# Differential attention: the low part of q in a doubled 128-row layout for the second pass of the score product

## The chip, the cores and the metric

The kernel runs on one core of a Trainium2 chip. The metric is the device time of one execution in microseconds (us); lower is better. Five engines work side by side and meet only through semaphores: TensorE (PE, with its weight loads listed as PEld), VectorE (DVE), ScalarE (ACT), GpSimd (POOL) and SyncE (SP, which issues most DMAs).

## What is computed

The reference is a four-layer trunk over 512 latent and 256 context tokens of width 1024. Layers 0 and 3 mix tokens with a short gated convolution, layer 1 with windowed attention, layer 2 with differential attention; each is followed by a gated convolutional feed-forward. Only layer 2's attention is touched here. It has 8 heads, each with two queries and two keys (index c) of 64 channels and one value of 128:

```python
s = jnp.einsum("bqhcd,bkhcd->bhcqk", q_j, keys, preferred_element_type=F32) * scale
p = jax.nn.softmax(s, axis=-1)
a = (p[:, :, 0] - lam * p[:, :, 1]).astype(vals.dtype)
o = jnp.einsum("bhqk,bkhe->bqhe", a, vals)
return rmsnorm(o, sub_g) * (1.0 - lam_init)
```

The 512 latent queries read 768 keys (512 latent, 256 context).

## The kernel before

All products run in the matmul type fp32r. To keep float32 accuracy each operand is split into a high part (the value cast to fp32r) and a low part (the value less the high part), and a product is the sum of high by high, high by low and low by high, three matmuls into one PSUM tile (`mm3`, lines 160 to 162). Where the contraction has only 64 channels, as in the scores, two of the three are put into one matmul of 128 rows.

That is what `diff_attn` does. `kT` holds, for each head and each c, a 128-row block with the 768 keys along the free axis: rows 0 to 63 carry one part of the key and rows 64 to 127 the other (high then low for c = 0, low then high for c = 1). `qprep(hd, tt)` makes the matching stationary operands for one head and one block of 128 queries. ACT copies the two high parts, each twice (`qst`, line 949), POOL forms the two low parts (line 950), PE transposes three 128x128 blocks into the PSUM tile `pqt` (line 953), and ACT copies them to `qT` (line 955): block 0 is the high part of query 0 doubled, block 1 that of query 1 doubled, block 2 the two low parts stacked, each in the 64 rows where the key's high part lies.

`scores(v)` (v is a head and a half of the queries, 16 in all, two query blocks each) then makes four score tiles `psS` [128 queries, 768 keys], 64 in the whole layer. A tile takes four matmuls: 512 keys by the 128-row high operand (line 979), the same keys by the 64-row low operand (line 980), and both again for the last 256 keys. Behind a tile come the row maximum on DVE (line 982), the exponential with its row sum on ACT (line 984), and after both c of a query block the scaling and the sum of the two on POOL (lines 993 and 994, the second listed under helper line 156). The PSUM pool has two buffers for `psS` and four of one bank for everything else.

`values(v)` transposes the combined probabilities on PE (line 1008), splits them on ACT and DVE (lines 1013 and 1014) and multiplies them with the values (`pO`, lines 160 to 162). `finish` normalizes a head (`oss` line 1041, `ops` line 176) and `out_proj` adds its output product (`pd`, lines 160 to 162 and 430). `timeline` weaves these generators; the order in which each engine then runs its instructions is fixed at build time by the scheduler of the language. PE, DVE, ACT and POOL take their instructions in that order.

`setup` makes two identity matrices, `ident` in float32 and `identr`, a cast of it to fp32r (lines 203 to 206).

Of the kernel before, what the change touches and what calls it, by code (L numbers as in the profile page):

```python
# [9 lines left out]
F32 = mybir.dt.float32  # L10
F32R = mybir.dt.float32r
AF = mybir.ActivationFunctionType
ALU = mybir.AluOpType
# [32 lines left out]
class Trunk:  # L46
# [1 line left out]
        self.tc, self.nc, self.A, self.out, self.stop = tc, tc.nc, A, out, stop  # L48
        self.xside = "left"

    # ---------------------------------------------------------------- weights
    def plan_weights(self):
        A = self.A
        w = []
# [55 lines left out]
        return hi, lo  # L110

    def prefetch(self, n):
        """Splits the next n weights, one a step, and lifts the limit."""
        for _ in range(n):
            if len(self.wready) < self.wpos + 5:
                self._split(True)
            self.wlimit = max(self.wlimit, len(self.wready))
            yield
# [10 lines left out]
        self.wready[i] = None  # L129
        return r  # L130

    # ---------------------------------------------------------------- helpers
    def ps(self, name):
        return self.pp.tile([P, 1024], F32, name=name, tag="ps", bufs=2)

# [40 lines left out]
            self.nc.tensor.matmul(ps[:, t * P:(t + 1) * P], r[:, t:t + 1].to_broadcast([P, P]), self.ident,  # L176
                                  start=True, stop=True)

    # ---------------------------------------------------------------- setup
    def setup(self, es):  # L180
        tc, nc, A = self.tc, self.nc, self.A
        self.cp = cp = es.enter_context(tc.tile_pool(name="const", bufs=1))
        self.pp = es.enter_context(tc.tile_pool(name="psum", bufs=1, space=PSUM))
        self.WR, self.WS = 3, 5
        self.wpool = es.enter_context(tc.tile_pool(name="w", bufs=1))

        pk = cp.tile([P, self.A["pack"].shape[1]], F32, name="pack")
        nc.sync.dma_start(pk, self.A["pack"])
        pos = 0

        def take(*dims):
            nonlocal pos
            n = math.prod(dims)
            v = pk[:, pos:pos + n]
            pos += n
            if len(dims) == 2:
                return v.rearrange("p (a b) -> p a b", b=dims[1])
            return v

        craw = take(KC, 2)  # L200
        self.cpair = cp.tile([P, KC, 2], F32, name="csilu")
        nc.scalar.activation(self.cpair, craw, AF.Silu)
        self.ident = cp.tile([P, P], F32, name="ident")
        make_identity(nc, self.ident)
        self.identr = cp.tile([P, P], F32R, name="identr")
        nc.vector.tensor_copy(self.identr, self.ident)
        self.ones = cp.tile([P, P], F32, name="ones")
        nc.gpsimd.memset(self.ones, 1.0)
        self.mhalf = cp.tile([P, 8], F32, name="mhalf")
        nc.gpsimd.memset(self.mhalf, -0.5)  # L210

        self.ada_b = [take(6, KC) for _ in range(DEPTH)]
        self.g1 = [take(KC) for _ in range(DEPTH)]
        self.g2 = [take(KC) for _ in range(DEPTH)]
        self.fcw = [take(NF, 3) for _ in range(DEPTH)]
        self.fcb = [take(NF) for _ in range(DEPTH)]
        self.scw = {l: take(KC, 3) for l in (0, 3)}
        self.sink = take(16)
        self.subln = take(1)
        self.mods = {}  # L220
        for l in range(DEPTH):
            for s in ((0, 1) if l < 3 else (0,)):
                self.mods[l, s] = cp.tile([P, 6, KC], F32, name=f"mod{l}_{s}")
        hL = [cp.tile([P, SEQ], F32, name=f"hL{k}") for k in range(KC)]
        self.hC2 = [cp.tile([P, 2, CTX], F32, name=f"hC{k}") for k in range(KC // 2)]
        hC = [self.hC2[k // 2][:, k % 2, :] for k in range(KC)]
        self.h = {0: hL, 1: hC}
# [4 lines left out]
        for k in range(KC):  # L232
            self.tc.keep_in_program_order(self.nc.sync.dma_start(self.h[0][k], self.A["x"][k]))

    # ---------------------------------------------------------------- ada
    def ada_vecs(self, l, m):
        return (0, 1) if l < 2 or (l == 2 and m < 2) else (0,)

    def ada_first(self):
        """Shift and scale of the first norms: a chunk of channels at a time, straight on the tensor engine."""  # L240
        nc = self.nc
        for j in range(KC):
            if j in EARLY:
# [62 lines left out]
            if next(self.ada, "end") == "end":  # L306
                break

    # ---------------------------------------------------------------- norm
    def norm_steps(self, l, s, second, first):  # L310
        """RMS norm and modulation of one stream: a step for the square of each chunk, then the rest.
        The first norms scale the chunks by the statistics before the modulation is there."""
        nc = self.nc
        sid, T, off = s
        xp = self.xp
# [67 lines left out]
            if k % 2 or first:  # L383
                yield

    # ---------------------------------------------------------------- pair structure
    def project(self, src, xn, parts, name, acc=None, split=False):
        """Projects some parts of the streams; acc is what an earlier call for other parts returned."""
        if acc is None:
            if split:  # L390
                out = {sid: self.pb(name) for sid, _, _ in parts}
            else:
                ps = self.ps(name)
                out = {0: ps[:, :SEQ], 1: ps[:, SEQ:TOK], "all": ps}
            acc = self.get_w(src), out
        (wh, wl), out = acc
        for s in parts:
            sid, T, off = s
            o = out[sid][:, off:off + T]
            for k in range(KC):  # L400
                xh, xl = xn[s][k]
                w = slice(k * P, (k + 1) * P)
                self.mm3(o, wh[:, w], wl[:, w], xh, xl, k == 0, k == KC - 1)
        return acc

    def phase_start(self, srcs, xn, regions):
        """The first projections of a phase leave the last part of the streams to the end."""
        n = PRM["nb"] if len(regions) == 2 else PRM["nl"]
        self.pre = [self.project(src, xn, parts_of(regions)[:-1], f"pre{i}", split=i >= 2) for i, src in enumerate(srcs[:n])]

# [20 lines left out]
                    yield  # L431

    def begin(self, s, first=False):
        """The norm of stream s for the phase that follows, if it takes part there."""
        if self.next is None or s not in parts_of(self.next[1]):
            return iter(())
        if self.xn_next is None:
# [3 lines left out]
        return self.norm_steps(self.next[0], s, self.next[2], first)  # L441

    def boundary(self, seq, gate, before=()):
        """The last down products, stream by stream, woven with the norms of the next phase."""
        prev = list(before)
        for s, units, ws, last in seq:
            nrm = self.begin(s) if last else iter(())
# [12 lines left out]
                pass  # L460

    def timeline(self, tasks, rate):
        """Interleaves generators: each task (begin, end, steps, generator) takes its steps evenly over its slots,
        and the filler takes rate steps a slot."""
        live = []
        tasks = sorted(tasks, key=lambda t: t[0])
        at, due, end = 0, 0.0, max(t[1] for t in tasks)
# [61 lines left out]

    @staticmethod  # L530
    def pair_order(n):
        """Units go up and down in groups, each going down while the next goes up; the last four go down together."""
        order = []
        for g in range(0, n - 2, GRP):
            order += [("up", c) for c in range(g, g + GRP)]
# [69 lines left out]
        gate = {sid: self.mods[l, sid][:, 2, :] for sid, _, _ in streams}  # L605
        self.pairs(KC, up, A[f"l{l}_sc_out"], gate, streams, ticks)

    # ---------------------------------------------------------------- attention pieces
    def rope_table(self, l, which, yt):
        """Gain, and cosine and sine with the gain in them, of one of q and k."""  # L610
        nc, A = self.nc, self.A
        g = yt.tile([P, 2, HD], F32, name=f"gain{l}{which}")
        nc.sync.dma_start(g, A[f"l{l}_gain"][:, "qk".index(which)])
# [58 lines left out]
                mm(o, xh, wl[:, w], start=False, stop=k == KC - 1)  # L672
            post(tt, o)

    # ---------------------------------------------------------------- layer 1 mixer
    def window_gqa(self, xn):
        nc, A = self.nc, self.A
        yc = self.tc.tile_pool(name="y1", bufs=1, side=self.yside)
# [203 lines left out]
        self.boundary([(H1, final[H1], ws[1], True)], gate, [nrm, nrm0])  # L882
        mc.__exit__(None, None, None)

    # ---------------------------------------------------------------- layer 2 mixer
    def diff_attn(self, xn):
        nc, A = self.nc, self.A
        yc = self.tc.tile_pool(name="y2", bufs=1, side=self.yside)
# [54 lines left out]
            yield  # L943

        def qprep(hd, tt):
            st = xb.tile([P, 3, 2, HD], F32R, name="qst", tag="qst", bufs=2)
            qc = (hd % 4) * P
            q3 = qraw[hd // 4, tt][:, qc:qc + P].rearrange("p (c d) -> p c d", c=2)
            self.cpy("st", st[:, 0:2], q3[:, :, None, :].to_broadcast([P, 2, 2, HD]))
            self.tt("stl", st[:, 2], q3, st[:, 0:2, 0, :].bitcast(F32), ALU.subtract)  # L950
            pt = self.pb("pqt")
            for c in range(3):
                self.tr(pt[:, c * P:(c + 1) * P], st[:, c].rearrange("p a d -> p (a d)"))
            qT = xb.tile([P, 3, P], F32R, name="qT", tag="qT", bufs=2)
            self.cpy("qT2", qT, pt[:, :384].rearrange("p (c t) -> p c t", c=3))
            return qT

        def scores(v):
# [9 lines left out]
            for n in range(2):  # L968
# [4 lines left out]
                pts = []  # L973
                for c in range(2):
                    s = self.ps("psS")
                    hs = slice(c * HD, c * HD + HD)
                    for a, b in ((0, 512), (512, 768)):
                        kt = kT[hd // 4][:, 2 * (hd % 4) + c, a:b]
                        nc.tensor.matmul(s[:, a:b], qT[:, c, :], kt, start=True, stop=False)  # L979
                        nc.tensor.matmul(s[:, a:b], qT[hs, 2, :], kt[hs], start=False, stop=True)  # L980
                    nm = self.small(1, "nm")
                    nc.vector.tensor_reduce(nm, s[:, :TOK], axis=AX.X, op=ALU.max, negate=True)
                    p = xb.tile([P, TOK], F32, name="pP", tag="P", bufs=6)
# [119 lines left out]
        self.boundary([(s, *self.last, True) for s in (H0, H1)], gate)  # L1103
        mc.__exit__(None, None, None)

    # ---------------------------------------------------------------- whole
    def run(self):
        tc, nc = self.tc, self.nc
        es = ExitStack()
# [183 lines left out]
```

## Time and profile before

| | |
|---|---|
| Time, median of 3 runs | 3337.18 us (3334.94 to 3341.43) |
| Span of the profiled execution, first to last instruction | 3339.3 us |
| Time of the profiled execution itself | not listed apart from its span |
| Mean granted TensorE clock | 0.972 of full |
| Score, softmax and value stage of layer 2 | about 2135 to 2365 us of the span |

A profile row of a timeline gives the start, the busy time, the engine, the line of the kernel, the operation, the tiles (out<-in), the shape and how many instructions are merged. Busy times of PE overlap, because a matmul is counted until its result is written; the distance from one start to the next is what a matmul costs the queue. In brackets stands the idle time of the engine before the row and what ended it; "issue" means that nothing seen in the profile did.

### The profile page before, as it was taken

How to read it: one execution, taken by the hardware profiler on the slowest of the kernel's cores; microseconds unless marked ns; L12 is line 12 of the kernel's file. 1: busy time of each engine (PE TensorE's matmuls, PEld its weight loads, DVE VectorE, ACT ScalarE, POOL GpSimd, SP SyncE). 2: the span in 40 equal slices, each digit the busy share in tenths (PEclk: the TensorE clock that was granted, in tenths of full speed). 3: DMA queues.
4: the chain of work that ended last, by engine and by line, in shares of the span. 5: the costliest groups of instructions: out<-in, count | busy, mean ns of one | idle time of the engine just before them, and what ended most of it. 6: DMA issues, size and time to landing. Idle time of an engine off the chain costs nothing.

```text
span 3339.3 us, 53917 instructions
## 1 busy us (share of the span) xinstructions
PE 3272.2 (98%) x22364; PEld 2979.7 (89%) x22364; DVE 2207.4 (66%) x3278; ACT 1127.0 (34%) x1888; POOL 686.3 (21%) x578
## 2 busy tenths in 40 slices
PE   8999999999998999999999999999999999999999
PEld 7999999989986778999999987677899999999999
DVE  5775887786565676676666576366687765565555
ACT  4113322222333565422222243356432323242222
POOL 2132223211132333111000134255211110010000
PEclk9999999999996899899999999899999999999999
DMA  6431443442110000333333112401265532222322
GB/s 226 139 108 52 152 132 110 134 132 77 52 65 19 14 21 6 102 108 113 110 127 112 60 54 79 142 29 54 68 202 161 179 112 89 95 89 84 101 89 76
DMA packets 105237, 323.29 MB, mean 97 GB/s; under 512 B 12576, under 2 KB 27552, under 8 KB 104992
## 3 DMA queue, kind: packets, MB, share of 16 engines
q1 hardware_dynamic: 100512, 313.26, 29.0%
q0 software_dynamic: 4480, 6.58, 0.9%
q8 instruction: 176, 2.88, 0.3%
q14 instruction: 69, 0.57, 0.1%
HBM read 311.26 MB, written 8.53 MB: 96 GB/s over the span
## 4 chain that ended last, share of the span: by engine, by line
PE 93%; DVE 4%; ACT 1%; DMA 1%; issue 1%; POOL 0%; SPq 0%; ACTq 0%; DVEq 0%; POOLq 0%
PE pd L160 8%; PE pd L161 8%; PE pd L162 8%; PE pa L161 6%; PE pa L160 6%; PE pa L162 6%; PE pg L160 6%; PE pg L162 6%; PE pg L161 6%; PE pj L670 3%; PE pj L671 3%; PE pj L672 3%; PE psS L980 2%; PE pO L826 2%; PE pPT L816 1%; PE psS L979 1%
## 5 line engine op out<-in xcount | busy, mean ns | idle before, releaser
L108 ACT CAST wh<-wr 128x1024 fp32r<-128x1024 f32 x380 | 392.2, 1049 | 1282.1 <-issue 524.9
L109 DVE TENSOR_TENSOR wl<-wr,wh 128x1024 fp32r<-128x1024 f32 x380 | 497.9, 1323 | 233.0 <-ACT wh L108 231.6
L160 PE MATMUL pd<-mh,wh 128*128 128x256 f32 (+1 forms) x1712 | 568.6, 333 | 9.9 <-DVE hC L430 9.2
L161 PE MATMUL pd<-ml,wh 128*128 128x256 f32 (+1 forms) x1712 | 564.1, 330 | 0.3 <-DVE ml L1057 0.3
L162 PE MATMUL pd<-mh,wl 128*128 128x256 f32 (+1 forms) x1712 | 563.7, 329 | 0.0
L430 DVE SCALAR_TENSOR_TENSOR hL<-pd,mod,hL 128x512 f32<-128x512 f32 (+1 forms) x512 | 335.6, 660 | 249.7 <-PE pd L162 248.2
L160 PE MATMUL pg<-xh,wh 128*128 128x256 f32 x1648 | 465.5, 282 | 1.5 <-ACT gp L575 1.5
L162 PE MATMUL pg<-xh,wl 128*128 128x256 f32 x1648 | 465.3, 282 | 0.0
L162 PE MATMUL pa<-xh,wl 128*128 128x256 f32 x1648 | 465.3, 282 | 0.0
L160 PE MATMUL pa<-xh,wh 128*128 128x256 f32 x1648 | 465.3, 282 | 0.0
L161 PE MATMUL pa<-xl,wh 128*128 128x256 f32 x1648 | 465.3, 282 | 0.0
L161 PE MATMUL pg<-xl,wh 128*128 128x256 f32 x1648 | 465.2, 282 | 0.0
L291 POOL PARTITION_ALL_REDUCE acc<-acc x34 | 222.9, 6587 | 1130.8 <-DVE acc L289 1130.8
L160 PEld LDWEIGHTS pd<-mh,wh 128*128 128x128 f32 x1712 | 325.8, 190 | 39.0 <-DVE hC L430 9.6
L162 PEld LDWEIGHTS pd<-mh,wl 128*128 128x128 f32 x1712 | 326.4, 191 | 30.8
L161 PEld LDWEIGHTS pd<-ml,wh 128*128 128x128 f32 x1712 | 326.4, 191 | 25.6 <-DVE ml L1057 0.5
L289 DVE SCALAR_TENSOR_TENSOR acc<-adaw,csilu,acc 128x1024 f32<-128x1024 f32 x238 | 297.8, 1279 | 47.5 <-DMA adaw<-l_ada_w 44.5
L160 PEld LDWEIGHTS pg<-xh,wh 128*128 128x128 f32 x1648 | 314.1, 191 | 5.5 <-ACT gp L575 1.7
L161 PEld LDWEIGHTS pg<-xl,wh 128*128 128x128 f32 x1648 | 314.0, 191 | 4.3
L162 PEld LDWEIGHTS pg<-xh,wl 128*128 128x128 f32 x1648 | 314.2, 191 | 2.1
L160 PEld LDWEIGHTS pa<-xh,wh 128*128 128x128 f32 x1648 | 314.6, 191 | 0.1
L161 PEld LDWEIGHTS pa<-xl,wh 128*128 128x128 f32 x1648 | 314.6, 191 | 0.1
(234 smaller groups left out, 6311.9 us busy)
## 6 DMA issues: line engine op xcount, KB each, us to landing
adaw<-l_ada_w SPq DMA_DIRECT2D x176, 512.0 KB, 3.7
wr<-l_ffn_up SPq DMA_DIRECT2D x176, 512.0 KB, 3.6
wr<-l_ffn_down SPq DMA_DIRECT2D x88, 512.0 KB, 3.6
wr<-l_sc_in SPq DMA_DIRECT2D x48, 512.0 KB, 3.6
wr<-l_da_qkv SPq DMA_DIRECT2D x24, 512.0 KB, 3.9
adaf<-l_ada_first SPq DMA_DIRECT2D x16, 512.0 KB, 5.7
wr<-l_sc_out SPq DMA_DIRECT2D x16, 512.0 KB, 3.6
wr<-l_wa_qkv SPq DMA_DIRECT2D x12, 512.0 KB, 3.8
```

The costliest lines, as they stand in the source:

```text
L108: keep(self.nc.scalar.copy(hi, raw))
L109: keep(self.nc.vector.tensor_tensor(lo, raw, hi.bitcast(F32), ALU.subtract))
L160: mm(ps, wh, xh, start=first, stop=False)
L161: mm(ps, wh, xl, start=False, stop=False)
L162: mm(ps, wl, xh, start=False, stop=last)
L289: keep(nc.vector.scalar_tensor_tensor(acc[v], raw, c, acc[v], ALU.mult, ALU.add))
L291: nc.gpsimd.partition_all_reduce(acc[v], acc[v], P, bass.bass_isa.ReduceOp.add)
L430: nc.vector.scalar_tensor_tensor(hk, ps, gate[sid][:, oc:oc + 1], hk, ALU.mult, ALU.add)
L670: mm(o, xh, wh[:, w], start=k == 0, stop=False)
L671: mm(o, xl, wh[:, w], start=False, stop=False)
L672: mm(o, xh, wl[:, w], start=False, stop=k == KC - 1)
L826: nc.tensor.matmul(po, vw, t, start=n == 1 and i == 0, stop=n == len(keys) and i == 1)
```

## The change

`qprep` makes the low parts in the same doubled form as the high parts: POOL writes 128x256 elements in place of 128x128, PE transposes four blocks in place of three, and ACT copies 512 columns in place of 384. Blocks 2 and 3 of `qT` are now the low part of query 0 and of query 1, each in both halves of the rows. `scores` uses them over all 128 rows of `kT`, so that the product of the low parts is added to the score too. Apart from that `setup` no longer keeps a float32 identity: it builds one in a scratch tile, casts it to `identr`, and reads `identr` as float32 where `ident` was read. Each of the two `qst` buffers and each of the two `qT` buffers grows by 512 bytes a partition; the dropped identity frees 512. The diff also removes comments and docstrings, left out here.

```diff
@@ setup
-        self.ident = cp.tile([P, P], F32, name="ident")
-        make_identity(nc, self.ident)
+        eye = self.ntmp("eye")[:, :P]
+        make_identity(nc, eye)
         self.identr = cp.tile([P, P], F32R, name="identr")
-        nc.vector.tensor_copy(self.identr, self.ident)
+        nc.vector.tensor_copy(self.identr, eye)
+        self.ident = self.identr.bitcast(F32)
@@ qprep
-            st = xb.tile([P, 3, 2, HD], F32R, name="qst", tag="qst", bufs=2)
+            st = xb.tile([P, 4, 2, HD], F32R, name="qst", tag="qst", bufs=2)
...
-            self.cpy("st", st[:, 0:2], q3[:, :, None, :].to_broadcast([P, 2, 2, HD]))
-            self.tt("stl", st[:, 2], q3, st[:, 0:2, 0, :].bitcast(F32), ALU.subtract)
+            q4 = q3[:, :, None, :].to_broadcast([P, 2, 2, HD])
+            self.cpy("st", st[:, 0:2], q4)
+            self.tt("stl", st[:, 2:4], q4, st[:, 0:2].bitcast(F32), ALU.subtract)
             pt = self.pb("pqt")
-            for c in range(3):
+            for c in range(4):
                 self.tr(pt[:, c * P:(c + 1) * P], st[:, c].rearrange("p a d -> p (a d)"))
-            qT = xb.tile([P, 3, P], F32R, name="qT", tag="qT", bufs=2)
-            self.cpy("qT2", qT, pt[:, :384].rearrange("p (c t) -> p c t", c=3))
+            qT = xb.tile([P, 4, P], F32R, name="qT", tag="qT", bufs=2)
+            self.cpy("qT2", qT, pt.rearrange("p (c t) -> p c t", c=4))
@@ scores
-                    hs = slice(c * HD, c * HD + HD)
                     for a, b in ((0, 512), (512, 768)):
                         kt = kT[hd // 4][:, 2 * (hd % 4) + c, a:b]
                         nc.tensor.matmul(s[:, a:b], qT[:, c, :], kt, start=True, stop=False)
-                        nc.tensor.matmul(s[:, a:b], qT[hs, 2, :], kt[hs], start=False, stop=True)
+                        nc.tensor.matmul(s[:, a:b], qT[:, 2 + c, :], kt, start=False, stop=True)
```

## Rows read from the trace of the kernel before

**Rows 1.** The page's busy shares: us, share of the span, instructions.

```profile
PE 3272.2 (98%) x22364; PEld 2979.7 (89%) x22364; DVE 2207.4 (66%) x3278; ACT 1127.0 (34%) x1888; POOL 686.3 (21%) x578
```

**Rows 2.** Windows of layer 2's attention: length, busy by engine, granted clock, DMA share, GB/s.

```profile
2135.00:2160.00 25.00, 20.20 (x46) 10.26 (x46) 9.83 (x16) 10.65 (x24) 11.11 (x15) 0.55 0.50 159
2160.00:2200.00 40.00, 39.37 (x159) 27.71 (x159) 19.13 (x36) 22.33 (x49) 20.71 (x21) 0.73 0.08 20
2200.00:2350.00 150.00, 148.43 (x782) 108.10 (x783) 100.98 (x170) 88.28 (x190) 83.33 (x81) 1.00 0.14 41
```

**Rows 3.** Waits from 2200 to 2350 us: total, times, longest.

```profile
DVE nm L982 <- PE psS L980: 23.6, 33, 2.1
PE oss L1041 <- ACT osq L1037: 1.6, 2, 0.8
```

**Rows 4.** Timeline of PE around one score tile at full clock.

```profile
2200.59 0.48 PE L979 MATMUL psS<-kT,qT 128*128 128x512 f32 x1
2201.01 0.49 PE L980 MATMUL psS<-kT,qT 64*128 64x512 f32 x1
2201.43 0.39 PE L979 MATMUL psS<-kT,qT 128*128 128x256 f32 x1
2201.74 0.38 PE L980 MATMUL psS<-kT,qT 64*128 64x256 f32 x1
2202.05 0.45 PE L165 MATMUL pqt<-identr,qst 128*128 128x128 f32 x3
2202.34 0.35 PE L160 MATMUL pO<-aTh,vhl 128*128 128x256 f32 x1
2202.53 0.28 PE L161 MATMUL pO<-aTl,vhl 128*128 128x256 f32 x1
2202.65 0.28 PE L162 MATMUL pO<-aTh,vl 128*128 128x256 f32 x1
```

**Rows 5.** Timeline of the weight loads (PEld) in the same stretch.

```profile
2201.01 0.18 PEld L980 LDWEIGHTS psS<-kT,qT 64*128 64x128 f32 x1 [0.25 <-issue]
...
2202.53 0.19 PEld L162 LDWEIGHTS pO<-aTh,vl 128*128 128x128 f32 x1
```

**Rows 6.** Timeline of PE: two matmuls of 512 columns with 128 rows.

```profile
2288.31 0.39 PE L160 MATMUL pd<-mh,wh 128*128 128x512 f32 x1
2288.54 0.40 PE L161 MATMUL pd<-ml,wh 128*128 128x512 f32 x1
```

**Rows 7.** Timeline of PE at half clock: two score tiles' first matmuls, two of 128 rows.

```profile
2154.36 0.79 PE L979 MATMUL psS<-kT,qT 128*128 128x512 f32 x1
...
2156.83 0.79 PE L979 MATMUL psS<-kT,qT 128*128 128x512 f32 x1
...
2167.36 0.41 PE L160 MATMUL pO<-aTh,vhl 128*128 128x256 f32 x1
2167.57 0.41 PE L161 MATMUL pO<-aTl,vhl 128*128 128x256 f32 x1
```

**Rows 8.** Groups of ACT from 2200 to 2350 us: busy, mean ns, idle before.

```profile
L1013 ACT CAST aTh<-pPT 128x512 fp32r<-128x512 f32 x33 | 19.3, 588 | 13.4 <-PE pPT L1008 13.1
L151 ACT CAST qT<-pqt 128x384 fp32r<-128x384 f32 x22 | 10.6, 481 | 16.0 <-PE pqt L165 16.0
```

**Rows 9.** Groups of POOL from 2200 to 2350 us.

```profile
L156 POOL TENSOR_TENSOR pP<-pP 128x768 f32<-128x768 f32 x23 | 42.1, 1830 | 1.3
L156 POOL TENSOR_TENSOR qst<-qraw,qst 128x128 fp32r<-128x128 f32 x16 | 7.4, 461 | 20.6 <-ACT qst L151 20.5
```

**Rows 10.** Timelines of ACT and PE: a PSUM buffer's release and its next use.

```profile
2258.23 0.21 ACT L984 ACTIVATION_READ_ACCUMULATOR pP<-psS,nm 128x1 f32 x1
...
2258.49 0.50 PE L979 MATMUL psS<-kT,qT 128*128 128x512 f32 x1
```

**Rows 11.** Windows of layer 1's attention, columns as in rows 2.

```profile
1030.00:1045.00 15.00, 15.00 (x39) 9.41 (x39) 6.12 (x16) 5.13 (x14) 2.71 (x4) 0.50 0.00 0
1165.00:1180.00 15.00, 14.75 (x90) 11.43 (x90) 11.90 (x28) 9.21 (x23) 5.14 (x6) 1.00 0.00 1
```

## The prediction on record

> **What bounds the kernel now.** I read the page's busy shares first: PE is busy 98% of the span and nothing else is near it [rows 1], so whatever shortens PE's queue anywhere should shorten the whole, if the queue doesn't start to wait. Then the windows of the stage that the change touches. From 2200 to 2350 us PE is busy 148.4 of 150 us at full clock, with DVE at 67%, ACT at 59% and POOL at 56%; the 65 us before that run partly at half clock (granted 0.55 and 0.73) [rows 2]. From these shares 44 of the 65 us are at the lower level: (1 - 0.55) / 0.5 of 25 us and (1 - 0.73) / 0.5 of 40 us. Then the waits of the 150 us: DVE waits 23.6 us for score tiles, while the largest wait of PE for another engine is 1.6 us [rows 3]. So in this stretch the other engines run behind PE, and PE runs behind nothing but its own queue.
>
> Busy time of PE tells little about what an instruction costs, so I read starts. One score tile takes the queue from 2200.59 to 2202.05, 1.46 us, in steps of 0.42, 0.42, 0.31 and 0.31 us [rows 4]. Elsewhere a matmul of 256 columns and 128 rows takes a step of 0.12 us [rows 4] and one of 512 columns 0.23 us [rows 6], each with a new weight block. The four of a score tile would be 0.23 + 0.23 + 0.12 + 0.12 = 0.70 us at that pace. More than half of what a score tile costs is thus something that other matmuls don't pay. The weight loads say what: the load for a full-height matmul starts a whole step ahead of its own matmul (2202.53 against 2202.65), while the 64-row load starts with its matmul at 2201.01 after 0.25 us in which the loader waited for nothing that the profile shows [rows 4, 5]. The load takes the same time in both (0.18 and 0.19 us) [rows 5]; it is its overlap that is lost, on the way into 64 rows and on the way back.
>
> The Trainium skill has two rules on this, and they disagree. TensorEngine Tiling, Key Properties, says that changing the tiling mode drains the engine; the idle loader of rows 5 agrees, and by that rule the sum is the one below. TensorE: Matmul & The Clock Gate, in its part on packing small matmuls and its closing table, says that a weight load overlaps a running matmul only where the row groups differ, and that a small-K matmul takes as long as a full one; by that the change would buy nothing. The full-height loads that do start early [rows 4, 5] speak against it; its time stands among the rivals.
>
> **The change part by part.**
>
> Score matmuls, full clock. All four of a tile become full height, so each alternates weight blocks as the rows of 0.12 and 0.23 us do. 1.46 - 0.70 = 0.76 us a tile. Of the 64 tiles 53 start at full clock, 45 of them in the 150 us: 53 x 0.76 = 40.3 us. Both ends: 0 if the cost doesn't go away, 0.76 if it goes wholly. I take the upper end, as the new instructions are the same form as the rows that don't pay.
>
> Score matmuls, half clock. Eleven tiles start there. Two neighbours are 2.47 us apart with nothing else between them, and a 256-column step is 0.21 us, so a 512-column one some 0.42 [rows 7]: 2.47 - 2 x 0.42 - 2 x 0.21 = 1.21 us, 13.3 us in all.
>
> One transpose more for each of 32 query blocks. Three take 0.29 us of the queue [rows 4], so 0.10 us each, 0.2 at half clock: 32 x 0.10 and some more, 3.6 us, on PE's queue and paid.
>
> ACT copies 512 columns to qT instead of 384. The 512-column copy of the same kind takes 588 ns against 481 [rows 8]: 0.11 us, 3.4 us over 32. POOL subtracts 256 columns instead of 128. Between 461 ns for 128 and 1830 ns for 768 columns [rows 9] lie 2.14 ns a column, so 0.27 us more, 8.8 us over 32. Both hide in the idle time of engines that are 59% and 56% busy [rows 2]. If the cover goes, a late qT stops the score matmuls that are queued behind it on PE; then up to 12 us are paid.
>
> The first product of the low parts costs no matmul of its own; it rides in rows that stood empty. The identity in a scratch tile: the same build and the same cast, before any matmul; nothing, and if exposed less than 1 us. The queues of the DMAs are not touched. The scheduler may order some instructions differently, as four of its inputs grow; I put that at 3 us either way and at zero in the sum.
>
> Sum on PE's queue: 40.3 + 13.3 - 3.6 = 50 us less.
>
> What comes back as waits. A score tile needs the buffer of the tile two before it, released by the exponential. PE gets there 2 x 0.76 us earlier, while the release comes only 0.76 us earlier, so that margin shrinks by 0.76 us. In the timeline 3 of the 45 tiles of the 150 us have less than that, the tightest 0.05 us (release at 2258.44, use at 2258.49) [rows 10]; the first eight tiles of the stage wait already. Other margins (split probabilities for pO, the late qT) shrink too. DVE's 101 us must now fit in 150 - 45 x 0.76 + 23 x 0.10 = 118 us, 86% [rows 2]; layer 1's attention shows DVE at 79% (11.90 of 15 us) while PE is still 98% busy [rows 11], but nothing shows 86%. I let this stretch end at 123 us, with DVE at 82%: a gain of 27 us. For the 65 us before it: 8 x 0.76 + 13.3 - 1.3 = 18 us on the queue, of which I give back 3, as the first tiles wait in turn for ACT. 27 + 15 = 42 us.
>
> What follows the stage is fed from the same queue and moves up whole. The span of the profiled execution, 3339.3 us, lies inside the runs (3334.9 to 3341.4), so what lies around it can't be told from their spread, and I set the 42 us against the median: 3337.2 - 42 = 3295 us.
>
> **The rivals.**
>
> The queues of the other engines hold it (gain between 12 and 35 us, 3302 to 3325). If DVE can't be pressed beyond 70 to 75%, the 150 us become 144 to 135, a gain of 6 to 15, with 6 to 15 from the start of the stage. For it: DVE serves score maxima, splits and residual sums in one fixed order, and a tight buffer exists [rows 10]. Against: PE waits on nobody in that stretch now [rows 3], and layer 1 reaches 79% [rows 11].
>
> The penalty isn't the row count (3340 us, no change). If the missing overlap belonged to the score tiles for another reason, such as the way that they read kT or write PSUM, the change would only add its transposes, 3.6 us, less than can be told. It is also what the Trainium skill's rule on overlap (TensorE: Matmul & The Clock Gate) would give. Against it: pO and pd accumulate into PSUM and alternate weights in the same manner at 0.12 and 0.23 us [rows 4, 6].
>
> The clock falls (slower). Layer 1's attention ran at half clock for 15 us on end although PE was shown 100% busy [rows 11]. New waits on PE could hold this stage there too. At half clock a step of 0.12 us is 0.21 [rows 4, 7], so a stretch of queue work grows by some 0.75 of itself: the gain of 42 us is gone when 42 / 0.75 = 56 us of the work now done at full clock runs at half, and all of the 118 us there gives 3295 + 88 = 3383 us. Against it: the same columns in less time leave PE's array busier on average than now, when the clock is full.
>
> The clock rises earlier. For the same reason the 44 us at the lower level may get shorter; the queue is full in most of it [rows 2]. Cutting 15 to 20 us of it gives 7 to 10 us more, 3285 us and below.
>
> **How the numbers follow.** The forecast, 35 to 53 us less (3284 to 3302), 0.66; the queues hold it 0.20; an earlier clock on top of the forecast (3274 to 3284) 0.07; no penalty removed 0.04; the clock falls 0.03. A tell from no change takes 0.2%, 6.7 us, so faster is 0.66 + 0.20 + 0.07 = 0.93, the same 0.04, slower 0.03. The range for 8 in 10 runs from 3280, taking in half of the earlier clock, to 3317, taking in most of the held queues.
>
> **What would show it right or wrong.** Right: 128 rows at both lines of the score matmuls; one tile's four starts 0.7 us long; weight loads that begin a step ahead of their matmul; the stage some 42 us shorter, with DVE above 80% in its middle; POOL's low part near 0.73 us and ACT's qT near 0.59 us, with PE hardly waiting for either. Wrong: steps still at 0.42 and 0.31 us (the penalty was something else), new PE waits for the exponential or for qT of more than 10 us in sum (the queues), or a granted clock below 1.00 in the middle of the stage.

## The result and the profile after

The changed kernel takes 3287.47 us (3281.69 to 3290.60, 4 runs) against 3336.06 us of the kernel before (3323.54 to 3341.43, 4 runs). The ratio is 0.986 with a 95% interval of 0.984 to 0.988, which makes it 47 us faster (40 to 53). The forecast was 42 us less, 3295 us, in a range of 3280 to 3317. The profiled execution took 3290.6 us with a span of 3288.8 us, so 1.8 us lie around the span.

The page of the kernel after, busy shares, to set beside [rows 1]:

```profile
PE 3216.7 (98%) x22396; PEld 2969.3 (90%) x22396; DVE 2206.6 (67%) x3278; ACT 1128.7 (34%) x1888; POOL 696.1 (21%) x578
```

PE is busy 55.5 us less, with 32 instructions more. The other engines do what they did, and POOL 10 us more. (Line numbers are one higher in most of the file: 980 and 981 are the two passes, 165 is still the transpose.)

The timeline of PE after, two score tiles, one behind a matmul and one behind transposes:

```profile
2208.30 0.39 PE L980 MATMUL psS<-kT,qT 128*128 128x512 f32 x1
2208.53 0.39 PE L981 MATMUL psS<-kT,qT 128*128 128x512 f32 x1
2208.75 0.28 PE L980 MATMUL psS<-kT,qT 128*128 128x256 f32 x1
2208.87 0.28 PE L981 MATMUL psS<-kT,qT 128*128 128x256 f32 x1
2208.99 0.29 PE L160 MATMUL pO<-aTh,vhl 128*128 128x256 f32 x1
2209.12 0.28 PE L161 MATMUL pO<-aTl,vhl 128*128 128x256 f32 x1
...
2211.91 0.60 PE L1009 MATMUL pPT<-identr,pP 128*128 128x128 f32 x4
2212.26 0.49 PE L980 MATMUL psS<-kT,qT 128*128 128x512 f32 x1
2212.59 0.39 PE L981 MATMUL psS<-kT,qT 128*128 128x512 f32 x1
2212.82 0.28 PE L980 MATMUL psS<-kT,qT 128*128 128x256 f32 x1
2212.94 0.28 PE L981 MATMUL psS<-kT,qT 128*128 128x256 f32 x1
2213.05 0.28 PE L160 MATMUL pO<-aTh,vhl 128*128 128x256 f32 x1
```

Steps of 0.23, 0.22, 0.12 and 0.12 us make 0.69 in all, and 0.79 us behind transposes, where the first step is 0.33. Before, a tile behind a transpose took 1.46 us [rows 4]. The weight loads of the second tile, from PEld's timeline:

```profile
2212.36 0.19 PEld L981 LDWEIGHTS psS<-kT,qT 128*128 128x128 f32 x1
2212.59 0.19 PEld L980 LDWEIGHTS psS<-kT,qT 128*128 128x128 f32 x1
```

Each now starts a whole step ahead of its matmul (2212.36 against 2212.59, 2212.59 against 2212.82), with no idle time of the loader in front, as the full-height ones did before [rows 5].

The windows of the stage after (length, busy of PE, PEld, DVE, ACT, POOL, granted clock, DMA share, GB/s):

```profile
2130.00:2150.00 20.00, 14.20 (x60) 10.79 (x59) 11.03 (x16) 12.71 (x27) 12.18 (x14) 0.74 0.66 211
2150.00:2190.00 40.00, 35.69 (x256) 31.79 (x255) 32.10 (x58) 34.03 (x76) 34.84 (x34) 1.00 0.08 23
2190.00:2300.00 110.00, 105.50 (x712) 94.25 (x710) 90.22 (x149) 76.97 (x164) 78.05 (x70) 1.00 0.18 55
```

Three things differ from [rows 2]. The half clock is over by 2150: 0.26 of full speed is missing over 20 us, so some 10 us ran at half clock where 44 did. DVE is 82% busy from 2190 on, ACT and POOL 85 and 87% from 2150 to 2190. And PE has real gaps now: 35.7 of 40 us. From the first score matmul to the end of the last one the stage takes 166.2 us (2134.6 to 2300.8) in place of 211.9 (2137.8 to 2349.7).

The 45.8 us between the two can be laid out by adding up the steps of PE in the stage, with the time in which it waits set apart (us):

| | before | after |
|---|---|---|
| 64 score tiles | 103.0 | 53.0 |
| transposes of q (`pqt`) | 8.4 | 10.4 |
| all that stands between (`pPT`, `pO`, `oss`, `ops`, `pd`) | 95.3 | 90.6 |
| waits | 5.3 | 12.2 |

What PE waits for by name, from the view of waits (total, times, longest), first before over 2135 to 2350 us, then after over 2132 to 2302 us:

```profile
PE psS L979 <- ACT pP L984: 3.2, 2, 1.7
PE oss L1041 <- ACT osq L1037: 1.6, 2, 0.8
PE pqt L165 <- ACT qst L151: 1.0, 1, 1.0
PE psS L979 <- ACT qT L151: 0.6, 1, 0.6
PE pPT L1008 <- ACT qT L151: 0.6, 1, 0.6
```

```profile
PE psS L980 <- ACT pP L985: 7.3, 9, 1.7
PE oss L1042 <- ACT osq L1038: 3.9, 4, 1.2
PE pO L161 <- DVE aTl L1015: 1.0, 2, 0.5
PE pqt L165 <- ACT qst L151: 1.0, 1, 1.0
PE pqt L165 <- POOL qst L156: 0.5, 2, 0.3
```

That is 7.0 us before and 13.7 after (these stretches begin some us ahead of the first score matmul, so they hold a little more than the table). The largest is the one that was expected: a score tile waits for its PSUM buffer until the exponential has read it.

### The profile page after: what moved, and what is told of

The parts are those of the page before. It is cut to its first block, busy times and chain, and to the rows that moved or that the text cites. A ratio compares the mean times of both kernels' runs of the same rounds, so it can differ in the third digit from the quotient of the medians.

```text
span 3288.8 us, 53979 instructions
## 1 busy us (share of the span) xinstructions
PE 3216.7 (98%) x22396; PEld 2969.3 (90%) x22396; DVE 2206.6 (67%) x3278; ACT 1128.7 (34%) x1888; POOL 696.1 (21%) x578
## 4 chain that ended last, share of the span: by engine, by line
PE 92%; DVE 4%; ACT 2%; issue 1%; DMA 0%; POOL 0%; SPq 0%; ACTq 0%; DVEq 0%; POOLq 0%
PE pd L160 9%; PE pd L161 8%; PE pd L162 8%; PE pa L160 6%; PE pa L162 6%; PE pa L161 6%; PE pg L160 6%; PE pg L162 6%; PE pg L161 6%; PE pj L671 3%; PE pj L672 3%; PE pj L673 3%; PE pO L827 2%; PE pPT L817 1%; PE pre L161 1%; PE pre L160 1%
```

## The experiments

The theory was that the array stops at each change between 128 and 64 rows, because the weights for the next matmul can't be loaded ahead. The rivals: a 64-row matmul is slow by itself; the score tiles are slow for another reason; the scheduler's new order brought the gain; the other engines' queues hold the stage. Times are compared with runs of the kernel before on the same chip. A difference of one profile's stage may hold some us of clock, so stage and time are both given.

**Second pass over 64 rows again, all else of the change kept.**

```diff
-    nc.tensor.matmul(s[:, a:b], qT[:, 2 + c, :], kt, start=False, stop=True)
+    nc.tensor.matmul(s[:, a:b], qT[hs, 2 + c, :], kt[hs], start=False, stop=True)
```

> The changed kernel with everything kept (four doubled blocks, four transposes, the scratch identity) but the second pass again over 64 rows, so that the product of the low parts is left out. If the row height is what costs (theory: the array drains when a matmul of another height comes), the steps of a score tile go back to 0.42, 0.43, 0.31 and 0.31 us and the time to that of the kernel before plus the transposes, 3336 + 3.6 = 3340 us (3334 to 3346). If the gain came from the order in which the scheduler put the instructions after the change, the time stays near 3287 us.

Measured: 3335.49 us against 3333.71, ratio 1.0008 (0.9993 to 1.0023). The timeline of PE, one tile behind a matmul (lines 981 and 982 here):

```profile
2284.77 0.40 PE L981 MATMUL psS<-kT,qT 128*128 128x512 f32 x1
2285.09 0.50 PE L982 MATMUL psS<-kT,qT 64*128 64x512 f32 x1
2285.52 0.39 PE L981 MATMUL psS<-kT,qT 128*128 128x256 f32 x1
2285.84 0.38 PE L982 MATMUL psS<-kT,qT 64*128 64x256 f32 x1
2286.15 0.38 PE L160 MATMUL pO<-aTh,vhl 128*128 128x256 f32 x1
2286.37 0.28 PE L161 MATMUL pO<-aTl,vhl 128*128 128x256 f32 x1
```

The steps are back (0.32, 0.43, 0.32, 0.31), and with them the whole 47 us. The step behind the tile is long too, 0.22 us (2286.15 to 2286.37) where it is 0.13 in the changed kernel (2208.99 to 2209.12). The stage is 218.9 us long, 7 us more than before: it has the extra transposes, and it ran some 51 us at half clock in this execution, where the kernel before had 44. The time shows less of it. So the row height brought all of the gain, within the interval. What the change added beside it costs little. The order in which PE's instructions stand in this stage is much nearer to that of the changed kernel than to that of the kernel before, so the order did not bring the gain either.

**The four matmuls of a tile grouped by height, in the kernel before.**

```diff
     for a, b in ((0, 512), (512, 768)):
         kt = kT[hd // 4][:, 2 * (hd % 4) + c, a:b]
         nc.tensor.matmul(s[:, a:b], qT[:, c, :], kt, start=True, stop=False)
+    for a, b in ((0, 512), (512, 768)):
+        kt = kT[hd // 4][:, 2 * (hd % 4) + c, a:b]
         nc.tensor.matmul(s[:, a:b], qT[hs, 2, :], kt[hs], start=False, stop=True)
```

> The kernel before with the four score matmuls of a tile in another order: both high ones (512 and 256 keys), then both low ones of 64 rows. Nothing else differs. If the cost is paid at each change of row height, a tile has two changes in place of four: steps of about 0.23, 0.31, 0.23 and 0.31 us, 1.08 in place of 1.44 us, so 53 x 0.36 us at full clock and some 7 us in the eleven tiles at half clock, 3336 - 26 = 3310 us (3302 to 3318). If a 64-row matmul is slow by itself, the number of changes is of no account and the time stays at 3336 us (3331 to 3341).

Measured: 3309.66 us (3308.27 to 3310.34), ratio 0.9926 (0.9905 to 0.9948). The timeline of PE merges the pairs of one line (979 and 982 here):

```profile
2253.34 0.52 PE L979 MATMUL psS<-kT,qT 128*128 128x512 f32 x2
2253.78 0.62 PE L982 MATMUL psS<-kT,qT 64*128 64x512 f32 x2
2254.33 1.16 PE L176 MATMUL ops<-ident,rstd 128*128 128x128 f32 x8
```

0.44 us for the two high ones and 0.55 for the two low ones, 0.99 in all; the median over the 64 tiles, with those behind transposes, is 1.07 against 1.46 us before. Two changes fewer save 0.39 us, 0.19 to 0.20 us a change. The same matmuls, the same operands and the same number of 64-row instructions in another order give half of the gain: it is the change that is paid for. Nothing else moved: outside the tile all engines have the order of the kernel before, and each matmul still has a weight load of its own (128 of either height in the layer).

**All four matmuls over 64 rows** (the product of q's high part with the key's low part is left out).

```diff
-    nc.tensor.matmul(s[:, a:b], qT[:, c, :], kt, start=True, stop=False)
+    nc.tensor.matmul(s[:, a:b], qT[hs, c, :], kt[hs], start=True, stop=False)
```

> The kernel before with all four score matmuls over the 64 rows of the key's high part; this leaves the product of q's high part with the key's low part out. If the cost is paid at a change of height, it is paid on the way into a tile and on the way out only: about 1.08 us a tile as in the run with the matmuls grouped, 3310 us (3302 to 3318). If 64 rows are slow by themselves, all four steps are long (0.43, 0.43, 0.31, 0.31), 1.48 us a tile, and the time is 3336 to 3341 us.

Measured: 3301.10 us, ratio 0.990 (0.987 to 0.993), some 9 us below what was expected. One tile in the timeline of PE:

```profile
2252.65 0.50 PE L979 MATMUL psS<-kT,qT 64*128 64x512 f32 x1
2252.99 0.40 PE L980 MATMUL psS<-kT,qT 64*128 64x512 f32 x1
2253.22 0.28 PE L979 MATMUL psS<-kT,qT 64*128 64x256 f32 x1
2253.34 0.28 PE L980 MATMUL psS<-kT,qT 64*128 64x256 f32 x1
2253.55 0.55 PE L1008 MATMUL pPT<-ident,pP 128*128 128x128 f32 x3
```

Inside the tile the steps are 0.23 and 0.12 us, those of full-height matmuls [rows 4, 6]; only the first (0.34) and the last (0.21) are long. So 64 rows are not slow among their like. A tile takes 0.90 us in the median and not the 1.08 expected, because half of what a change costs lies in the step before it and half in the step behind it, and here two of these four steps belong to the tile's neighbours. At full clock a 256-column matmul that stands before a tile takes a step of 0.21 us in the median, and one that stands behind it 0.22, both 0.12 elsewhere. With these a change costs 0.20 us in this run, and the same comes out of the grouped run and of the kernel before when the step behind the tile is added.

That leaves the shorter time to explain, which the four runs give loosely (3292.61 to 3307.61 us). Where the two tiles of one query block follow each other directly, one reads rows 0 to 63 and the other rows 64 to 127, and their matmuls run at the same time, two starts being merged in each row:

```profile
2209.36 0.52 PE L979 MATMUL psS<-kT,qT 64*128 64x512 f32 x2
...
2210.28 0.39 PE L160 MATMUL pO<-aTh,vhl 128*128 128x256 f32 x1
```

The two tiles take 0.92 us together. This happens in a few places only; by an estimate from their starts it is worth some 4 us, about what this stage is shorter than that of the grouped run (178.0 against 182.6 us).

One weight load of the single tile above, from PEld's timeline:

```profile
2252.76 0.19 PEld L980 LDWEIGHTS psS<-kT,qT 64*128 64x128 f32 x1
```

It starts 0.23 us ahead of its own matmul (2252.99), while the tile's first matmul runs on the same rows. The Trainium skill (TensorE: Matmul & The Clock Gate, closing table) says that a small-K matmul takes as long as a full one: these steps agree. The Trainium skill's rule in the same page's part on packing small matmuls, that weight loads overlap a running matmul only where the row groups differ, does not hold here: the load at 2252.76 overlaps a matmul on its own rows, and so do the full-height ones. The Trainium skill's TensorEngine Tiling, Key Properties, gives the rule that fits all three runs: a change of tiling mode drains the engine.

**The same in layer 1.** Its scores have 160 matmuls of 64 rows. The high half of q goes by POOL into a block whose other half stays zero, and the key block of two heads is then read over all rows; one buffer fewer in the ring of probabilities makes room.

```diff
+    qz = [xb.tile([P, 4, P], F32R, name=f"qz{half}") for half in range(2)]
...
+    nc.gpsimd.tensor_copy(qz[half][rows], qT[rows].bitcast(F32))
...
-    nc.tensor.matmul(o, qT[hs, i, :], kT2[0][hs, j // 2, b0 * P:b0 * P + nl], start=False, stop=False)
+    nc.tensor.matmul(o, qh[:, i, :], kT2[0][:, j // 2, b0 * P:b0 * P + nl], start=False, stop=False)
...
-    nc.tensor.matmul(o, qT[hs, i, :], kT2[1][hs, j // 2, :], start=False, stop=True)
+    nc.tensor.matmul(o, qh[:, i, :], kT2[1][:, j // 2, :], start=False, stop=True)
```

> The changed kernel, and in layer 1's attention the 160 score matmuls of 64 rows get 128 rows too: the high half of q is copied by POOL into a block whose other half is zero, and the key block of two heads is read over all rows. The ring of probability tiles there has 9 buffers in place of 10 to make room. If a change of height costs some 0.36 us for each 64-row matmul there as well (0.19 before it and 0.19 behind it), PE's queue loses 58 us; with a fifth to a quarter of it given back as waits the time is 3287 - 45 = 3242 us (3230 to 3258). If DVE and ACT, 65 to 79% busy in that stage, hold it, 3265 to 3287 us. If the row height is not the cost, 3287 us or somewhat more for POOL's copies.

Measured: 3245.66 us (3244.08 to 3249.29), ratio 0.9737 to the kernel before (0.9715 to 0.9758). That is 42 us below the changed kernel and inside what was expected if the height is the cost (3230 to 3258). The view of waits of PE in layer 1's stage, its three largest, and that stage's window:

```profile
PE pqt L165 <- DVE qs L156: 8.6, 6, 4.5
PE pPT L824 <- POOL pP L808: 6.8, 10, 1.5
PE psS L782 <- ACT pP L795: 6.5, 8, 1.5
```

```profile
1015.00:1270.00 255.00, 217.10 (x1415) 188.49 (x1415) 195.00 (x447) 166.90 (x398) 112.95 (x144) 0.91 0.06 20
```

PE is busy 217 of 255 us now; DVE's share is 76%. Some of the gain is clock: the stage is granted 0.91 here, and 0.85 in the changed kernel (1015 to 1310 us). Here the zero rows carry nothing, so it is the height of the instruction that matters and not what stands in the rows.

**The doubling copy on DVE in place of ACT.** Three runs of the changed kernel load or relieve one of the engines behind PE.

```diff
-st='A'
+st='D'
```

> The changed kernel with the copy that doubles q's high part (32 of them, 0.41 us each) on DVE in place of ACT. ACT is 97 to 100% busy between 2160 and 2170 us of the changed kernel, and PE waits 7.3 us for exponentials in the stage. If ACT's queue is what PE waits for there, the stage from the first score matmul to the end of the last one, 166.2 us, gets 3 to 6 us shorter. If it is the length of the chain from score tile to released buffer, or DVE, it stays within 2 us or gets longer.

Measured: 3285.51 us, ratio 0.9852 (0.9836 to 0.9869), not to be told from the changed kernel; the stage is 168.3 us. Either ACT's load is not what PE waits for, or DVE takes back what ACT gives; this run can't tell which.

**POOL's low parts formed twice.**

```diff
+            self.tt("stl", st[:, 2:4], q4, st[:, 0:2].bitcast(F32), ALU.subtract)
             self.tt("stl", st[:, 2:4], q4, st[:, 0:2].bitcast(F32), ALU.subtract)
```

> The changed kernel with POOL forming the low parts twice (the second writes the same again): 32 x 0.73 us more on POOL, 23 us. The step of the prediction that costs POOL's growth at nothing says that it hides in POOL's idle time: a stage of 166.2 us give or take 2. If POOL's queue is in fact near the path, a tenth or more of the 23 us shows: 169 us and more.

Measured: 3297.31 us (3296.49 to 3298.88), ratio 0.9889 (0.9875 to 0.9904), stage 172.5 us: 6.3 of the 23 us show. The first 50 us of its stage by the windows:

```profile
2133.00:2183.00 50.00, 41.03 (x249) 34.63 (x248) 33.42 (x57) 36.67 (x80) 44.98 (x48) 0.92 0.21 68
```

POOL is 90% busy there. Its cover is not whole.

**ACT's copy to qT twice.**

```diff
+            self.cpy("qT2", qT, pt.rearrange("p (c t) -> p c t", c=4))
             self.cpy("qT2", qT, pt.rearrange("p (c t) -> p c t", c=4))
```

> The changed kernel with ACT copying the four transposed blocks to qT twice: 32 x 0.59 us more on ACT, 19 us. If ACT's growth hides as predicted, the stage stays at 166.2 us give or take 2. If ACT is what PE waits for in the first part of the stage, where it is 97 to 100% busy for a while, some 3 to 8 of the 19 us show: 169 to 174 us.

Measured: 3293.47 us (3285.93 to 3298.72), ratio 0.9875 (0.9856 to 0.9894), stage 169.9 us: 3.7 of the 19 us show, a fifth, at the low end of what the theory of an ACT near its limit gave. The interval reaches that of the changed kernel, so the time alone doesn't settle it.

## Why the prediction was right

**The cost and its place.** Right, and shown by undoing it: with 64 rows again the gain is gone, with two changes of height in place of four half of it comes, with no change inside the tile the steps are those of any matmul. The two rivals on the cause, no penalty from the row count and the Trainium skill's rule on overlap, fall by the same three runs. The cost is also larger than one tile's rows show: a change takes 0.20 us, half of it in the step behind, so a tile with four of them lengthens the step of whatever matmul follows it.

**Full-clock tiles, 0.76 us each.** Mis-sized, by two things that work against each other. Inside the tile it is 0.67 to 0.69: 1.46 to 0.79 us in the median, or 1.38 (in the run with 64 rows again, 2284.77 to 2286.15) to 0.69 behind a matmul. The row that the prediction took for before stood behind a transpose, the steps that it set against it stood behind matmuls; the 0.1 us behind a transpose stays. What it left out is the step behind the tile, 0.10 us where a matmul follows. Waits apart, the 53 tiles that it set at 40.3 us gave 35.4, and some 3 us more came from the 30 `pO` and `pd` steps behind a tile at full clock.

**Eleven tiles at half clock, 13.3 us.** The term assumed that they stay at half clock; only five of them did. (By the clock of the trace before two more tiles touch it, one as it ends and one in a short stretch near 2196 us.) Waits apart they gave 14.5 us. The 64 tiles together gave 50.0 us, where the two terms had 53.6.

**The transposes.** Four take 0.37 us (2210.07 to 2210.44 in the timeline after) where three took 0.29 [rows 4]: 0.08 us, 2.6 us over 32; by the table 2.0, where 3.6 had been set.

**Waits that come back, 8 us.** By name 13.7 against 7.0 us: 6.7, and 6.8 by the table. The place was right, the PSUM buffers of the score tiles, as was DVE's share of 82%. The reading that the first eight tiles wait already was not: before, two waits for the exponential stand in the whole stage, after, nine. The rival of the held queues would have needed 15 us and more by the prediction's own sum (50 less 35), and DVE went well past the 75% that it set as a limit. Its bounds do not add up either: 6 to 15 us twice is 12 to 30, not 35.

**ACT's and POOL's growth hidden.** The sizes were right. The instructions on qT and on qst after, one group of ACT and one of POOL (ns minimum, median, maximum; first and last start; 24 of ACT's 56 are layer 1's):

```profile
L151 ACT CAST qT<-pqt x56: 574/586/623, 1020.9 to 2294.2; 128x512 fp32r<-128x512 f32 x56
L156 POOL TENSOR_TENSOR qst<-qraw,qst x16: 734/741/1282, 2199.5 to 2284.1; 128x256 fp32r<-128x256 f32 x16
```

That it is wholly hidden is not borne out for POOL: of what is added on top of the change, a quarter shows in the stage, and the time is longer too. Of what is added to ACT a fifth shows in the stage, but the time doesn't settle it. If the change's own 3.4 and 8.8 us show by the same shares, which no run tried, they cost some 3 us (an estimate), of which the waits above hold a part. The scratch identity was not tried by itself; the run with 64 rows again holds it too and shows no cost of it that can be told.

**The clock.** The prediction gave an earlier rise 0.07 as a case of its own. It came: 44 us at half clock became 10. Part of the gain therefore came by a way that the sum did not hold. It shows in the eleven tiles above and in the matmuls between the tiles, which the prediction set at no change and which take 4.7 us less, though the stage now holds six `pd` matmuls more. Before, some 13 us of them ran at half clock; at the full-clock steps of the same groups they would take some 7 us (an estimate). How this shares the 4.7 us with the steps behind the tiles, and with the new order, was not followed further.

The first 50 us of the stage by kernel; the kernel before, 64 rows again, all 64 rows, grouped, changed:

```profile
2137.00:2187.00 50.00, 46.19 (x142) 28.52 (x142) 21.07 (x34) 23.36 (x54) 21.71 (x25) 0.59 0.21 68
```

```profile
2123.00:2173.00 50.00, 46.68 (x153) 28.52 (x153) 21.53 (x36) 25.02 (x55) 25.37 (x27) 0.62 0.21 69
```

```profile
2137.00:2187.00 50.00, 45.85 (x211) 37.52 (x212) 32.20 (x53) 31.67 (x72) 31.26 (x34) 0.66 0.26 86
```

```profile
2137.00:2187.00 50.00, 45.54 (x196) 31.66 (x197) 28.92 (x47) 29.67 (x67) 30.90 (x33) 0.70 0.25 81
```

```profile
2134.00:2184.00 50.00, 42.03 (x265) 36.44 (x266) 35.45 (x61) 38.72 (x86) 40.34 (x40) 0.90 0.26 83
```

The granted clock goes from 0.59 to 0.90 while PE's busy time in them falls from 46.2 to 42.0 us. One trace is a loose measure of it: layer 1, which has the same code in all kernels but one, ran between 65 and 96 us at half clock in their traces. But the two groups do not touch. In the four kernels with 64-row tiles the stage ran 31 to 51 us at half clock; in the changed kernel and the four runs built on it that keep its full-height tiles, 8 to 14 us. So the full-height tiles bring the earlier rise. By what they bring it is not shown: a faster flow of matmuls does not put the five windows in order, as the run with all 64 rows starts more matmuls than the grouped one (211 against 196) at a lower clock (0.66 against 0.70). The rival in which the clock falls did not come: from 2150 us on it is 1.00.

So the stage gained 45.8 us where the forecast had 42, and the nearness is in part luck. The tiles gave 3.6 us less than the sum; the transposes cost 1.6 and the waits 1.2 us less than set; the matmuls between the tiles, set at nothing, gave 4.7. By the ratio the time fell some 5 us below the forecast, which is inside what 4 runs of each kernel can tell.

## What to carry to other kernels

Read what a matmul costs from the distance between starts, and hold matmuls of another row height against those of the same columns: here each change between 64 and 128 rows cost 0.20 us at full clock, nearly as much as a matmul of 512 columns, and half of it stood in the step behind the change, outside the tile. Give every matmul of a stage one height, if need be with zero or doubled rows; where there is no room, group them by height. When a queue gets shorter, ask which buffers it reaches earlier, and what clock it then runs at.

## What the runs showed of the hardware that was not expected

A matmul behind a transpose takes a step some 0.1 us longer than behind another matmul (0.33 against 0.23 us for 512 columns, 2212.26 and 2208.30 of the timeline after), at the same row height.

Matmuls of 64 rows follow one another at the pace of full ones (0.23 and 0.12 us), with loads of 64 rows at the same place in between.

Two 64-row tiles on different halves of the rows ran at the same time when they stood next to each other: both in 0.92 us (2209.36 to 2210.28 in the run with all 64 rows), where one takes 0.90.

PE shown 92% busy went with a granted clock of 0.59 and 142 matmuls in 50 us, and 84% with 0.90 and 265: the busy share says little about how fast the queue moves.
